# Low-part score products and prompt scores over all 128 rows of the TensorE array, in a two-layer hybrid attention step

## The chip, the cores and the metric

The kernel runs on one core of a Trainium2 chip. The metric is the device time of one execution in microseconds (us). TensorE (PE) multiplies matrices, VectorE (DVE), ScalarE (ACT) and GpSimd (POOL) work on elements, SyncE (SP) issues the DMAs. Every engine works through its own instructions in order and waits on semaphores of the others.

## The reference

One step of a two-layer network over 1024 sample tokens and 128 prompt tokens, 1024 wide. The part that matters here is the differential attention of four heads, each with two maps of 64 dims:

```
def _diff_attention(q, k, v, lam, subln_w, lam_init):
    s = jnp.einsum('bhqmd,bhkmd->bhmqk', q, k,
                   preferred_element_type=jnp.float32) * (HEAD_DIM ** -0.5)
    p = jax.nn.softmax(s, axis=-1)
    a = p[:, :, 0] - lam * p[:, :, 1]
    o = jnp.einsum('bhqk,bhke->bhqe', a, v.astype(jnp.float32))
    o = (o * lax.rsqrt(jnp.mean(jnp.square(o), axis=-1, keepdims=True) + RMS_EPS)
         * subln_w.astype(jnp.float32) * (1.0 - lam_init))
    return o.astype(v.dtype)
```

The samples' 1024 queries attend to 1152 keys (1024 of their own and 128 cached ones). The prompt's 128 tokens attend to themselves alone. Around it stand one input projection for all branches, a Fourier branch, a gated spatial branch, an output projection and a layer norm.

## The kernel before

Each layer has four stages: the start (normalization and first projections), the attention, the rest of the local branches, and the output projection. To keep the accuracy of 32-bit numbers at the faster rate of the rounded type, an operand is split into a rounded high part and a low part (the difference), and a product is made of three: high by high, high by low, low by high.

For the scores the two maps of 64 dims are laid out so that 128 rows hold two of these at once. K holds, for map 1, the high part in rows 0 to 63 and the low part in rows 64 to 127, and the other way round for map 2. `pack` prepares the queries of two tiles (256 queries) in a tile Q: ScalarE copies the high part of map m into both halves of Q[:, m] (L597 to L600), so that one product over 128 rows (L610) gives high by high and high by low. POOL then subtracts to get the low parts of both maps into one slice, Q[0:64, 2] and Q[64:128, 2] (L601, L602). The product low by high (L613) runs over the 64 rows of K that hold the high part.

`score` does this for one tile of 128 queries and one map: three products of 384 keys over 128 rows, then three over 64 rows, into the same PSUM tile S. VectorE takes the maximum (nm, L616) and ScalarE the exponentials (P, L618). With both maps there, `softmax_diff` joins them (POOL L562, DVE L563), `transpose` turns the result on PE (T, L628) and copies it (a, L631 and L632), and `values` multiplies by V (pv, L638). There are 2 layers x 4 heads x 8 tiles x 2 maps = 128 scores and 32 packs.

`prompt` runs once for each head. It has one product over 64 rows for each map (sp, L655), from qp and kp, which hold both maps one above the other.

PE's order is the order in which the code is written: `attention` is a generator, and between its steps `fill` and the streams put products of the input projection (z, L366), so that PE works while other engines finish. The other engines' orders are made by a scheduler with priorities. Rotation of a projected chunk of q or k uses tiles zz and sh (POOL L409, L410), K's low part is made by POOL (L419), weights' low parts by POOL (L347), the end of a head's rows in `finish_o` by POOL (msq, gs, L579 to L581) and DVE (L582). The next layer's modulation is summed by DVE (macc, L185) meanwhile.

Short-lived tiles share buffers by tags: tag "z" has three buffers, tag "Q" two.

Of the kernel before, what the change touches and what calls it, by code (L numbers as in the profile page):

```python
# [16 lines left out]
D = 1024  # L17
# [13 lines left out]
# PE time of other work that goes with each step of the attention of a head  # L31
# [15 lines left out]
# units of 128 columns of the input projection  # L47
# [3 lines left out]
# tags and counts of the short-lived tiles, by name  # L51
X_TAGS = {"wr": ("wraw", "woraw", "wada", "tabr", "mr", "ba"), "z": ("zz", "sh", "gt", "vT", "gmt", "gmg", "fot", "vs", "bd", "pqp", "ws", "kc", "vc", "Pp", "modacc"), "Q": ("Q", "bdr", "wsr", "h32"),
# [10 lines left out]
def backbone_step(ctx, tc, xs, xp, cT, w_ada, b_ada, w_in, w_out, ckT, cv, lamv, wf, wsT, bsT,  # L63
# [13 lines left out]
    # ---- tiles of the pools, by use  # L77
# [28 lines left out]
    # ---- constants  # L106
# [13 lines left out]
    cb = tX([128, 34], "cb")  # the conditionings; layer 0's biases of shift and scale; the subln weights  # L120
# [31 lines left out]
    # ---- adaLN modulation of one third (0 shift, 1 scale, 2 gate), for both conditionings  # L152
# [42 lines left out]
    # ---- layer norm over the free dimension of [128, D], in place  # L195
# [33 lines left out]
    def make_h(l, t, xn):  # L229
        """h^T of token tile t, split, from the normalized x [128 tokens, D]."""  # L230
# [20 lines left out]
    def make_h_pair(l, c, kp, xs3):  # L251
        """Two of the eight blocks of dims of h^T, for the three token tiles of a chunk."""
# [23 lines left out]
    def start(proj):  # L276
        """Layer 0's shift and scale by blocks of 256 dims; the first chunk of the input projection follows them."""
# [64 lines left out]
    # ---- weights  # L342
# [72 lines left out]
    def split_k(K, sl, src):  # L415
        # K[:, 0] = [hi of map 1; lo of map 1], K[:, 1] = [lo of map 2; hi of map 2]
# [82 lines left out]
    class Units:  # L499
        """A stream of dims-major units; the weights of the next ones are loaded ahead."""  # L500
# [9 lines left out]
        def gen(self, which, together=False, chunks=(0, 1, 2)):  # L510
            """The units one by one, or their chunks in turn."""
# [20 lines left out]
    class Stream:  # L532
        """Work to be interleaved with other work."""
# [14 lines left out]
        def until(self, *units):  # L548
            """Until these units are projected."""
# [8 lines left out]
    def softmax_diff(l, p1, p2, zz, name):  # L558
        """p1 <- p1 / z1 - lam * p2 / z2"""
# [10 lines left out]
    def finish_o(l, o, ms, sq, n, gs, sl):  # L570
        """gs[:, sl] <- RMS norm of o [128 dims, n tokens] * weight * gate"""
        pe.matmul(ms, lhsT=onesm, rhs=sq[:, :n], start=True, stop=True)
        dve.scalar_tensor_tensor(gs[:, sl], o, subs[:, l:l + 1], gs[:, sl], op0=ALU.mult, op1=ALU.mult)
        # r = (m + eps) ** -0.5 by logarithm, then a Newton step: r * (3 - (m + eps) * r * r) / 2
# [9 lines left out]
    # ---- attention: one pipeline over the heads and their tiles of 128 queries  # L584
    class Head:
# [7 lines left out]
        def pack(self, p):  # L593
            """Two tiles of queries: [hi; hi] of either map, and lo of both."""
            qr, qs = self.qr, slice(p * 256, p * 256 + 256)
            Q = self.Q = tX([128, 3, 256], "Q", F32R)
# [4 lines left out]
            pool.tensor_tensor(Q[0:64, 2], qr[0:64, qs], f(Q[0:64, 0]), op=ALU.subtract)  # L601
            pool.tensor_tensor(Q[64:128, 2], qr[64:128, qs], f(Q[64:128, 1]), op=ALU.subtract)  # L602
            return Q

        def score(self, Q, i, m, zz):
            S, K = psS(), self.K
            ql = slice((i % 2) * 128, (i % 2) * 128 + 128)
            r = slice(64 * m, 64 * m + 64)
            for n in range(3):
                pe.matmul(S[:, n, :CH], lhsT=Q[:, m, ql], rhs=K[:, m, n * CH:(n + 1) * CH],  # L610
                          start=True, stop=False)
            for n in range(3):
                pe.matmul(S[:, n, :CH], lhsT=Q[r, 2, ql], rhs=K[r, m, n * CH:(n + 1) * CH],  # L613
                          start=False, stop=True)
# [31 lines left out]
        def prompt(self):  # L646
            """The prompt attends to itself."""
# [3 lines left out]
            P = tX([128, 2, 128], "Pp")  # L651
            for m in range(2):
                S = psM((128, 128), "sp")
                r = slice(64 * m, 64 * m + 64)
                pe.matmul(S, lhsT=self.qp[r, :], rhs=self.kp[r, :], start=True, stop=True)  # L655
# [7 lines left out]
            aT = self.qp  # the queries are no longer needed  # L663
# [71 lines left out]
    # ---- the local branches  # L735
    def local_u(l):
# [6 lines left out]
        for ts in TG:  # L743
            z = yield from mm_tok(w, ts)
            t = tX([128, 2, 256], "gmt")[:, :len(ts)]
            g = tX([128, 2, 256], "gmg")[:, :len(ts)]
            silu_to(g, z, t)
            sl = ug[:, ts[0]:ts[-1] + 1]
            pool.tensor_tensor(sl, sl, g, op=ALU.mult)
# [22 lines left out]
    def local_f(l):  # L772
        ff = [tX((128, 4, 256), "ff") for _ in range(2)]
        fp = small([128, 1, 256], "fp", 1)
        res["f", l] = ff, fp
        w = load_w256(l, U_F)
        for ts in TG:
            z = yield from mm_tok(w, ts)
            t = ts[0] % 4
            act.activation(fp if ts[0] == 8 else ff[ts[0] // 4][:, t:t + 2], z, AF.Copy)  # L780
# [36 lines left out]
    def fourier_weights(l, j):  # L817
        """Block-diagonal channel DFTs times w_f, split: [hi, lo][cos, -sin]."""
# [25 lines left out]
    def fourier_prepare(l):  # L844
        """Sums and differences of the halves, tables and weights, all split."""
        ff, fp = res.pop(("f", l))
        # tables [hi, lo] of the odd and of the even frequencies
# [22 lines left out]
    def local_fourier(l):  # L870
# [4 lines left out]
        for j in range(2):  # L875
            cj = slice(j * 128, (j + 1) * 128)
            w, bd = fo[j], bdr[j]
            PQ = tW((128, 2, 2, 2, 256), "PQ")  # [hi, lo][cos, sin][even, odd]
            F = res["F", l, j] = tR(name="F")
            # the prompt  # L880
            sp_ = psS((128, 256), "dftp")
            pe.matmul(sp_, lhsT=fp[:, 0, cj], rhs=dftp, start=True, stop=True)
            pq = tX((128, 2, 256), "pqp", F32R)
            act.activation(pq[:, 0], sp_, AF.Copy)
            dve.tensor_tensor(pq[:, 1], sp_, f(pq[:, 0]), op=ALU.subtract)
# [13 lines left out]
            # the sine table's column of frequency 0 holds the cosines of frequency 512  # L899
# [5 lines left out]
            for q in range(2):  # L905
                for a, b in PASSES:
                    pe.matmul(uv[:, 2, 0:128], lhsT=bd[:, a, q], rhs=pq[:, b, q * 128:(q + 1) * 128],
# [9 lines left out]
            vs = tX((128, 2, 256), "vs")  # L917
            act.activation(vs, uv[:, 1].rearrange("p (e k) -> p e k", e=2), AF.Copy)
            act.activation(F[:, 512:513], uv[:, 2, 128:129], AF.Copy)
            act.activation(F[:, SEQ_S:], uv[:, 2, 0:128], AF.Copy)  # L920
            dve.tensor_tensor(F[:, 0:512].rearrange("p (k e) -> p e k", e=2), U, vs, op=ALU.add)
            dve.tensor_tensor(F[:, 1022:513:-2], U[:, 0, 1:], vs[:, 0, 1:], op=ALU.subtract)
            dve.tensor_tensor(F[:, 1023:512:-2], U[:, 1], vs[:, 1], op=ALU.subtract)
            dve.tensor_tensor(F, F, gsf[j], op=ALU.mult)

    def load_w_out(l):
        """The output projection's weights, split; in the order in which their places fall free."""
# [196 lines left out]
```

## Time and profile before

| | us |
|---|---|
| median of 3 runs | 1456.73 |
| lowest and highest | 1454.4 and 1459.6 |
| span of the profiled execution | 1457.9 |
| TensorE busy in it | 1386.1 |
| VectorE busy in it | 902.8 |
| GpSimd busy in it | 770.1 |
| ScalarE busy in it | 742.5 |

The profile gives the span of its one execution, from its first to its last instruction; the runs are timed apart from it. Busy times of the engines overlap, so they don't add up to the span. The mean granted clock of TensorE was 0.983 of full speed.

### The profile page before, as it was taken

What the parts mean: (1) busy time and instruction counts of PE and PEld (TensorE: products, weight loads), DVE (VectorE), ACT (ScalarE), POOL (GpSimd) and SP (SyncE); (2) the same over time, 40 slices, a digit from 0 to 9 for tenths busy, and PEclk for the clock granted to TensorE, in tenths of its full rate; (3) what the DMA queues carried; (4) which work ended last, traced back from release to release, by engine and by line L of the source; (5) the groups of instructions that cost most, each with busy time, mean ns of one, the idle gap of its engine ahead of it and who ended that gap; (6) DMA issues with size and microseconds to landing.
All of it is one profiled execution on the core that took longest, in us unless ns stands there. A gap on an engine that the chain in (4) does not pass through costs nothing.

```text
span 1457.9 us, 21131 instructions
## 1 busy us (share of the span) xinstructions
PE 1386.1 (95%) x8248; PEld 1220.4 (84%) x8248; DVE 902.8 (62%) x1351; ACT 742.5 (51%) x1370; POOL 770.1 (53%) x655
## 2 busy tenths in 40 slices
PE   7999999989899999999998999999899999999997
PEld 3688888888688899987888889888779999998787
DVE  5435566886867855345785555578765684434576
ACT  3466656556544345353556665665655544435321
POOL 2164665676563445236787675576574342533652
PEclk9999999999989999999999999999999999999999
DMA  9310011221221221354341100112100010126442
GB/s 340 136 34 31 19 33 46 65 74 32 81 70 32 88 62 50 107 187 149 123 157 46 50 21 29 48 33 89 62 33 7 25 46 30 35 84 211 151 130 91
DMA packets 56156, 114.42 MB, mean 78 GB/s; under 512 B 4972, under 2 KB 32492, under 8 KB 55928
## 3 DMA queue, kind: packets, MB, share of 16 engines
q1 hardware_dynamic: 56056, 113.07, 23.3%
q8 instruction: 65, 1.06, 0.3%
q14 instruction: 35, 0.29, 0.1%
HBM read 95.47 MB, written 17.58 MB: 78 GB/s over the span
## 4 chain that ended last, share of the span: by engine, by line
PE 69%; DVE 12%; ACT 6%; POOL 4%; issue 3%; DMA 2%; DVEq 0%; SPq 0%; POOLq 0%; ACTq 0%
PE z L366 21%; PE y L983 11%; PE zt L381 8%; PE pv L638 6%; PE S L613 5%; PE zt L386 4%; PE S L610 4%; PE T L628 3%; DVE macc L185 2%; PE dft L893 2%; DVE nm L616 1%; ACT P L618 1%; DMA wada<-in_w_ada_dram 1%; PE mres L191 1%; DVE rr L1000 1%
## 5 line engine op out<-in xcount | busy, mean ns | idle before, releaser
L366 PE MATMUL z<-H,w 128*128 128x384 f32 x2520 | 505.7, 348 | 15.7 <-DVE V L484 4.5
L366 PEld LDWEIGHTS z<-H,w 128*128 128x128 f32 x2520 | 437.4, 191 | 44.7 <-issue 26.5
L618 ACT ACTIVATE P<-S,nm 128x1152 f32<-128x1152 f32 x128 | 156.2, 1221 | 114.9 <-DVE nm L616 114.2
L616 DVE TENSOR_REDUCE nm<-S 128x1 f32<-128x1152 f32 x128 | 172.8, 1351 | 53.1 <-PE S L613 52.6
L381 PE MATMUL zt<-whi,H 128*128 128x256 f32 x1152 | 159.4, 286 | 2.3 <-ACT ug L741 2.1
L562 POOL TENSOR_SCALAR P<-P,rz,neglam 128x1152 f32<-128x1152 f32 x64 | 85.3, 1332 | 139.4 <-DVE rz L561 127.1
L381 PEld LDWEIGHTS zt<-whi,H 128*128 128x128 f32 x1152 | 145.6, 191 | 8.6 <-issue 5.2
L563 DVE SCALAR_TENSOR_TENSOR P<-P,rz 128x1152 f32<-128x1152 f32 x64 | 104.3, 1630 | 32.8 <-POOL P L562 32.6
L347 POOL TENSOR_TENSOR w<-wraw,w 128x1024 fp32r<-128x1024 f32 x36 | 91.5, 2541 | 59.0 <-ACT w L346 57.4
L638 PE MATMUL pv<-a,V 128*128 128x256 f32 x864 | 109.5, 284 | 5.1 <-ACT P L618 5.1
L638 PEld LDWEIGHTS pv<-a,V 128*128 128x128 f32 x864 | 106.9, 192 | 7.0 <-ACT P L618 7.0
L632 DVE TENSOR_TENSOR a<-T,a 128x1152 fp32r<-128x1152 f32 x64 | 86.6, 1353 | 36.4 <-ACT a L631 36.3
L613 PE MATMUL S<-K,Q 64*128 64x384 f32 x384 | 102.0, 372 | 0.0
L610 PE MATMUL S<-K,Q 128*128 128x384 f32 x384 | 91.1, 345 | 7.2 <-ACT P L618 3.4
L983 PE MATMUL y<-wob,mx 128*128 128x512 f32 (+1 forms) x342 | 87.0, 381 | 2.2 <-DVE rr L985 2.2
L613 PEld LDWEIGHTS S<-K,Q 64*128 64x128 f32 x384 | 60.8, 187 | 32.4 <-issue 29.4
L631 ACT ACTIVATE a<-T 128x1152 fp32r<-128x1152 f32 x64 | 72.3, 1130 | 28.3 <-PE T L628 27.4
L386 PE MATMUL zt<-wlo,H 128*128 128x256 f32 x576 | 83.3, 285 | 1.1 <-POOL wlo L347 1.1
L628 PE MATMUL T<-cs,P 128*128 128x128 f32 x576 | 74.8, 276 | 8.5 <-ACT P L618 8.5
L983 PE MATMUL y<-wo,mx 128*128 128x512 f32 (+1 forms) x342 | 80.5, 378 | 0.0
L628 PEld LDWEIGHTS T<-cs,P 128*128 128x128 f32 x576 | 67.6, 143 | 13.0 <-ACT P L618 9.2
L610 PEld LDWEIGHTS S<-K,Q 128*128 128x128 f32 x384 | 67.4, 191 | 12.9 <-ACT P L618 4.7
(215 smaller groups left out, 2374.9 us busy)
## 6 DMA issues: line engine op xcount, KB each, us to landing
wraw<-in_w_in_dram SPq DMA_DIRECT2D x52, 512.0 KB, 3.3
wada<-in_w_ada_dram SPq DMA_DIRECT2D x32, 512.0 KB, 3.7
wa<-in_w_ada_dram SPq DMA_DIRECT2D x8, 1024.0 KB, 12.4
woraw<-in_w_out_dram SPq DMA_DIRECT2D x16, 512.0 KB, 3.8
mr<-mix SPq DMA_DIRECT2D x18, 384.0 KB, 3.3
mix<-gs SPq DMA_DIRECT2D x8, 576.0 KB, 3.7
x<-rr SPq DMA_DIRECT2D x9, 512.0 KB, 3.2
xr<-x SPq DMA_DIRECT2D x9, 512.0 KB, 5.3
```

Source lines behind the costliest of these rows:

```text
L347: eng.tensor_tensor(lo, raw, f(hi), op=ALU.subtract)
L366: pe.matmul(z, lhsT=w[:, a, kt, :], rhs=Hc[c][:, b, kt, :], start=n == 0, stop=n == 23)
L381: pe.matmul(z[:, i, :], lhsT=Hc[c][:, a, kt, o:o + 128], rhs=w[0][:, kt, :], start=n == 0, stop=False)
L386: pe.matmul(z[:, i, :], lhsT=Hc[c][:, 0, kt, o:o + 128], rhs=w[1][:, kt, :], start=False, stop=kt == KT - 1)
L563: return dve.scalar_tensor_tensor(p1, p1, rz[:, 0:1], p2, op0=ALU.mult, op1=ALU.add)
L610: pe.matmul(S[:, n, :CH], lhsT=Q[:, m, ql], rhs=K[:, m, n * CH:(n + 1) * CH], start=True, stop=False)
L613: pe.matmul(S[:, n, :CH], lhsT=Q[r, 2, ql], rhs=K[r, m, n * CH:(n + 1) * CH], start=False, stop=True)
L616: dve.tensor_reduce(nm, S[:, :, :CH], axis=AX.XY, op=ALU.max, negate=True)
L618: act.activation(P.rearrange("p (c k) -> p c k", c=3), S[:, :, :CH], AF.Exp, bias=nm, accum_out=zz[:, m:m + 1])
L628: pe.transpose(T[:, kt // 3, kt % 3, :], a[:, kt * 128:(kt + 1) * 128], ident)
L638: pe.matmul(pv[:, 0, :], lhsT=self.V[:, a, kt, :], rhs=self.A[:, b, kt, :], start=kt == 0 and e == 0, stop=kt == 8 and e == 2)
L983: pe.matmul(z, lhsT=mx[:, a, k, :], rhs=wo[kt][b][:, ns], start=i == 0, stop=i == 23)
```

## The change

Q gets a fourth slice. The low part of each map is written into both halves of its own slice, by four POOL subtractions (L604) instead of two, and all six products of a score run over 128 rows (L613). The second three now also contain low by low, a term that was left out.

The prompt's queries get a tile qm of their own, in which each map's slice holds that map's 64 rows and zeros in the other 64: POOL clears it (L654) and copies the two halves (L657), and the products run over 128 rows of qm and kp (L660). qm takes a buffer of tag "z".

To make room, tiles of tag "z" shrink from 512 to 384 columns: gmt and gmg hold one token tile instead of two (nine groups of instructions instead of five), pqp and vs are split in two, fot moves to tag "Q", and the prompt's part of f goes into two small tiles.

```
         def pack(self, p):
...
-            Q = self.Q = tX([128, 3, 256], "Q", F32R)
+            Q = self.Q = tX([128, 4, 256], "Q", F32R)
...
-            pool.tensor_tensor(Q[0:64, 2], qr[0:64, qs], f(Q[0:64, 0]), op=ALU.subtract)
-            pool.tensor_tensor(Q[64:128, 2], qr[64:128, qs], f(Q[64:128, 1]), op=ALU.subtract)
+            for m in range(2):
+                r = slice(64 * m, 64 * m + 64)
+                for b in (0, 64):
+                    pool.tensor_tensor(Q[b:b + 64, 2 + m], qr[r, qs], f(Q[r, m]), op=ALU.subtract)
...
         def score(self, Q, i, m, zz):
...
-            r = slice(64 * m, 64 * m + 64)
-            for n in range(3):
-                pe.matmul(S[:, n, :CH], lhsT=Q[:, m, ql], rhs=K[:, m, n * CH:(n + 1) * CH],
-                          start=True, stop=False)
-            for n in range(3):
-                pe.matmul(S[:, n, :CH], lhsT=Q[r, 2, ql], rhs=K[r, m, n * CH:(n + 1) * CH],
-                          start=False, stop=True)
+
+            for e in (m, 2 + m):
+                for n in range(3):
+                    pe.matmul(S[:, n, :CH], lhsT=Q[:, e, ql], rhs=K[:, m, n * CH:(n + 1) * CH],
+                              start=e == m, stop=e != m)
...
         def prompt(self):
...
+            qm = tX([128, 2, 128], "qm")
+            pool.memset(qm, 0.0)
+            for m in range(2):
+                r = slice(64 * m, 64 * m + 64)
+                pool.tensor_copy(qm[r, m], self.qp[r])
             for m in range(2):
                 S = psM((128, 128), "sp")
-                r = slice(64 * m, 64 * m + 64)
-                pe.matmul(S, lhsT=self.qp[r, :], rhs=self.kp[r, :], start=True, stop=True)
+                pe.matmul(S, lhsT=qm[:, m], rhs=self.kp, start=True, stop=True)
...
     def local_u(l):
...
-            t = tX([128, 2, 256], "gmt")[:, :len(ts)]
-            g = tX([128, 2, 256], "gmg")[:, :len(ts)]
-            silu_to(g, z, t)
-            sl = ug[:, ts[0]:ts[-1] + 1]
-            pool.tensor_tensor(sl, sl, g, op=ALU.mult)
+            for i, t in enumerate(ts):
+                e, g = tX([128, 256], "gmt"), tX([128, 256], "gmg")
+                silu_to(g, z[:, i], e)
+                pool.tensor_tensor(ug[:, t], ug[:, t], g, op=ALU.mult)
```

The order of PE's instructions at the start of layer 0's attention, where z is the projection and S the score:

```order
 L366 MATMUL z<-H_113,w_592 128x384 x3
-L610 MATMUL S<-K,Q 128x384 x3
-L613 MATMUL S<-K,Q 128x384 x3
+L613 MATMUL S<-K,Q 128x384 x6
 L366 MATMUL z<-H_113,w_592 128x384 x6
-L610 MATMUL S<-K,Q 128x384 x3
-L613 MATMUL S<-K,Q 128x384 x3
+L613 MATMUL S<-K,Q 128x384 x6
```

The six products stay where the three and three stood.

POOL's order before the prompt of head 1 in layer 0, in the kernel before (Q from `pack`, sh and zz from the rotation, P from `softmax_diff`, K's low part, then `finish_o`):

```order
L601 TENSOR_TENSOR Q<-qr,Q 64x256
L602 TENSOR_TENSOR Q<-qr,Q 64x256
L409 TENSOR_TENSOR sh<-sh,rp 128x384
L410 TENSOR_TENSOR zz<-zz,rp 128x384
L562 TENSOR_SCALAR P<-P,rz,neglam 128x1152
L419 TENSOR_TENSOR K<-zz,K 64x384 x2
L409 TENSOR_TENSOR sh<-sh,rp 128x384
L410 TENSOR_TENSOR zz<-zz,rp 128x384
L579 TENSOR_TENSOR msq<-msq,sq 128x256
```

And the same place after the change:

```order
L604 TENSOR_TENSOR Q<-qr,Q 64x256 x4
L409 TENSOR_TENSOR sh<-sh,rp 128x384
L410 TENSOR_TENSOR zz<-zz,rp 128x384
L562 TENSOR_SCALAR P<-P,rz,neglam 128x1152
L419 TENSOR_TENSOR K<-zz,K 64x384 x2
L654 MEMSET qm 128x256
L409 TENSOR_TENSOR sh<-sh,rp 128x384
L410 TENSOR_TENSOR zz<-zz,rp 128x384
L657 COPY qm<-qp 64x128 x2
```

Two more subtractions stand ahead of everything, and the two copies of qm, for which the first sp on PE waits, stand behind the second rotation.

POOL's order at the start of layer 1's attention, in the kernel before (w is a weight unit's low part; K at the end is what the first score waits for):

```order
L601 TENSOR_TENSOR Q<-qr,Q 64x256
L409 TENSOR_TENSOR sh<-sh,rp 128x384
L410 TENSOR_TENSOR zz<-zz,rp 128x384
L602 TENSOR_TENSOR Q<-qr,Q 64x256
L347 TENSOR_TENSOR w_7327<-wraw,w_7327 128x1024
L601 TENSOR_TENSOR Q<-qr,Q 64x256
L409 TENSOR_TENSOR sh<-sh,rp 128x256
L410 TENSOR_TENSOR zz<-zz,rp 128x256
L602 TENSOR_TENSOR Q<-qr,Q 64x256
L347 TENSOR_TENSOR w_7688<-wraw,w_7688 128x1024
L419 TENSOR_TENSOR K<-zz,K 64x256 x2
```

And after the change:

```order
L604 TENSOR_TENSOR Q<-qr,Q 64x256 x2
L409 TENSOR_TENSOR sh<-sh,rp 128x384
L410 TENSOR_TENSOR zz<-zz,rp 128x384
L604 TENSOR_TENSOR Q<-qr,Q 64x256 x2
L347 TENSOR_TENSOR w_7413<-wraw,w_7413 128x1024
L604 TENSOR_TENSOR Q<-qr,Q 64x256 x2
L409 TENSOR_TENSOR sh<-sh,rp 128x256
L410 TENSOR_TENSOR zz<-zz,rp 128x256
L604 TENSOR_TENSOR Q<-qr,Q 64x256 x2
L347 TENSOR_TENSOR w_7778<-wraw,w_7778 128x1024
L419 TENSOR_TENSOR K<-zz,K 64x256 x2
```

Four more subtractions stand ahead of K; the rest has kept its order.

## Rows read from the trace of the kernel before

**Rows 1.** The page: span, busy time of each engine, chain by engine and line.
```profile
span 1457.9 us, 21131 instructions
...
PE 1386.1 (95%) x8248; PEld 1220.4 (84%) x8248; DVE 902.8 (62%) x1351; ACT 742.5 (51%) x1370; POOL 770.1 (53%) x655
...
PE 69%; DVE 12%; ACT 6%; POOL 4%; issue 3%; DMA 2%; DVEq 0%; SPq 0%; POOLq 0%; ACTq 0%
PE z L366 21%; PE y L983 11%; PE zt L381 8%; PE pv L638 6%; PE S L613 5%; PE zt L386 4%; PE S L610 4%; PE T L628 3%; DVE macc L185 2%; PE dft L893 2%; DVE nm L616 1%; ACT P L618 1%; DMA wada<-in_w_ada_dram 1%; PE mres L191 1%; DVE rr L1000 1%
```

**Rows 2.** Windows: length; PE, PEld, DVE, ACT, POOL busy; PE clock; DMA.
```profile
103.00:570.00 467.00, 447.96 (x2765) 399.12 (x2765) 322.60 (x452) 253.57 (x469) 252.51 (x216) 0.98 0.17 53
816.00:1262.00 446.00, 432.28 (x2727) 389.10 (x2726) 285.41 (x423) 245.50 (x459) 233.42 (x211) 1.00 0.12 37
317.20:320.60 3.40, 3.40 (x15) 3.40 (x13) 3.27 (x4) 3.34 (x7) 3.32 (x4) 0.50 0.00 0
846.60:850.00 3.40, 3.39 (x17) 2.90 (x18) 2.94 (x3) 1.75 (x5) 1.22 (x2) 1.00 0.00 0
```

**Rows 3.** Timeline of PE, layer 0: start, length, operation [wait before].
```profile
419.00 7.01 PE L366 MATMUL z<-H,w 128*128 128x384 f32 x39
425.85 0.68 PE L610 MATMUL S<-K,Q 128*128 128x384 f32 x3
427.19 2.35 PE L366 MATMUL z<-H,w 128*128 128x384 f32 x12
429.38 0.69 PE L610 MATMUL S<-K,Q 128*128 128x384 f32 x3
```

**Rows 4.** Timeline of PE at the prompt of head 1, layer 0.
```profile
248.52 1.15 PE L628 MATMUL T<-cs,P 128*128 128x128 f32 x9
249.60 0.48 PE L655 MATMUL sp<-kp,qp 64*128 64x128 f32 x2
250.01 1.83 PE L366 MATMUL z<-H,w 128*128 128x384 f32 x9
251.69 0.69 PE L610 MATMUL S<-K,Q 128*128 128x384 f32 x3
...
252.31 0.49 PE L655 MATMUL sp<-kp,qp 64*128 64x128 f32 x2
...
253.02 0.79 PE L366 MATMUL z<-H,w 128*128 128x384 f32 x3
```

**Rows 5.** Waits of PE, layer 0 and layer 1: us, times, longest.
```profile
PE T L628 <- ACT P L618: 4.2, 1, 4.2
...
PE pv L638 <- ACT P L618: 2.6, 3, 0.9
...
PE T L628 <- ACT P L618: 4.3, 1, 4.3
```

**Rows 6.** POOL's groups of instructions: count, busy us, mean ns, idle before.
```profile
L602 POOL TENSOR_TENSOR Q<-qr,Q 64x256 fp32r<-64x256 f32 x32 | 30.2, 945 | 6.8 <-ACT Q L599 3.8 <-ACT Q L600 1.7
L601 POOL TENSOR_TENSOR Q<-qr,Q 64x256 fp32r<-64x256 f32 x32 | 25.9, 811 | 77.3 <-ACT Q L597 77.3
L822 POOL MEMSET bd<- 128x256 f32 x4 | 1.2, 311 | 3.2 <-DVE gs L397 1.7 <-DVE fo L815 1.5
```

**Rows 7.** Timeline of POOL before that prompt.
```profile
245.33 1.30 POOL L562 TENSOR_SCALAR P<-P,rz,neglam 128x1152 f32<-128x1152 f32 x1 [0.82 <-DVE rz L561]
246.71 3.30 POOL L419 TENSOR_TENSOR K<-zz,K 64x384 fp32r<-64x384 f32 x2
...
251.06 1.02 POOL L410 TENSOR_TENSOR zz<-zz,rp 128x384 f32<-128x384 f32 x1
```

**Rows 8.** Timeline of POOL and of PE at the start of layer 1's attention.
```profile
814.71 2.40 POOL L347 TENSOR_TENSOR w<-wraw,w 128x1024 fp32r<-128x1024 f32 x1
817.19 1.53 POOL L419 TENSOR_TENSOR K<-zz,K 64x256 fp32r<-64x256 f32 x2
...
817.98 0.44 PE L610 MATMUL S<-K,Q 128*128 128x384 f32 x1 [0.57 <-POOL K L419]
```

**Rows 9.** Timeline of POOL, DVE and PE at a late T, layer 0.
```profile
302.42 1.61 POOL L602 TENSOR_TENSOR Q<-qr,Q 64x256 fp32r<-64x256 f32 x1
307.38 1.22 DVE L582 SCALAR_TENSOR_TENSOR gs<-msq,gs 128x256 f32<-128x256 f32 x1 [0.80 <-POOL msq L580]
308.52 5.36 DVE L185 SCALAR_TENSOR_TENSOR macc<-wada,csil,macc 128x1024 f32<-128x1024 f32 x2
316.55 1.62 PE L628 MATMUL T<-cs,P 128*128 128x128 f32 x9 [4.18 <-ACT P L618]
```

More of the change, by code (lines that the diff above doesn't have):

```diff
@@ L48 @@
 U_Q, U_K, U_V, U_G, U_F, U_GF, U_U, U_VM, U_GM = 0, 4, 8, 12, 16, 18, 20, 22, 24
-X_TAGS = {"wr": ("wraw", "woraw", "wada", "tabr", "mr", "ba"), "z": ("zz", "sh", "gt", "vT", "gmt", "gmg", "fot", "vs", "bd", "pqp", "ws", "kc", "vc", "Pp", "modacc"), "Q": ("Q", "bdr", "wsr", "h32"),
+X_TAGS = {"wr": ("wraw", "woraw", "wada", "tabr", "mr", "ba"), "z": ("zz", "sh", "gt", "vT", "gmt", "gmg", "vs", "bd", "pqp", "ws", "kc", "vc", "Pp", "qm", "modacc"), "Q": ("Q", "bdr", "wsr", "h32", "fot"),
           "sq": ("sq", "wft", "dftp", "msq", "bds", "cb")}
@@ L773, in local_f @@
         ff = [tX((128, 4, 256), "ff") for _ in range(2)]
-        fp = small([128, 1, 256], "fp", 1)
+        fp = [small([128, 128], n, 2) for n in ("qp", "kp")]
         res["f", l] = ff, fp
@@ L779, in local_f @@
             t = ts[0] % 4
-            act.activation(fp if ts[0] == 8 else ff[ts[0] // 4][:, t:t + 2], z, AF.Copy)
+            if ts[0] == 8:
+                for j in range(2):
+                    act.activation(fp[j], z[:, 0, j * 128:(j + 1) * 128], AF.Copy)
+            else:
+                act.activation(ff[ts[0] // 4][:, t:t + 2], z, AF.Copy)
     def local_gmlp(l):
@@ L881, in local_fourier @@
             sp_ = psS((128, 256), "dftp")
[L882 to L885, printed above, removed]
+            pe.matmul(sp_, lhsT=fp[j], rhs=dftp, start=True, stop=True)
+            pq = [tX((128, 256), "pqp", F32R) for _ in range(2)]
+            act.activation(pq[0], sp_, AF.Copy)
+            dve.tensor_tensor(pq[1], sp_, f(pq[0]), op=ALU.subtract)
             yield 500
@@ L906, in local_fourier @@
                 for a, b in PASSES:
-                    pe.matmul(uv[:, 2, 0:128], lhsT=bd[:, a, q], rhs=pq[:, b, q * 128:(q + 1) * 128],
+                    pe.matmul(uv[:, 2, 0:128], lhsT=bd[:, a, q], rhs=pq[b][:, q * 128:(q + 1) * 128],
                               start=n == 0, stop=n == 5)
@@ L916, in local_fourier @@
             U = uv[:, 0].rearrange("p (e k) -> p e k", e=2)
-            vs = tX((128, 2, 256), "vs")
-            act.activation(vs, uv[:, 1].rearrange("p (e k) -> p e k", e=2), AF.Copy)
+            vs = [tX((128, 256), "vs") for _ in range(2)]
+            for e in range(2):
+                act.activation(vs[e], uv[:, 1, e * 256:(e + 1) * 256], AF.Copy)
             act.activation(F[:, 512:513], uv[:, 2, 128:129], AF.Copy)
             act.activation(F[:, SEQ_S:], uv[:, 2, 0:128], AF.Copy)
-            dve.tensor_tensor(F[:, 0:512].rearrange("p (k e) -> p e k", e=2), U, vs, op=ALU.add)
-            dve.tensor_tensor(F[:, 1022:513:-2], U[:, 0, 1:], vs[:, 0, 1:], op=ALU.subtract)
-            dve.tensor_tensor(F[:, 1023:512:-2], U[:, 1], vs[:, 1], op=ALU.subtract)
+            for e in range(2):
+                dve.tensor_tensor(F[:, e:512:2], U[:, e], vs[e], op=ALU.add)
+            dve.tensor_tensor(F[:, 1022:513:-2], U[:, 0, 1:], vs[0][:, 1:], op=ALU.subtract)
+            dve.tensor_tensor(F[:, 1023:512:-2], U[:, 1], vs[1], op=ALU.subtract)
             dve.tensor_tensor(F, F, gsf[j], op=ALU.mult)
```

## Prediction

> **What bounds the kernel now.** I read the page's busy shares and its chain first. TensorE is busy for 95% of the span, the next engine for 62%, and 69% of the chain that ended last is TensorE's [rows 1]. The two score lines hold 9% of that chain (5 for L613, 4 for L610) and VectorE 12%. So in most places TensorE work taken away shortens the span, but at a wait for another engine it only lengthens the wait.
>
> Second come the windows of the two attentions, the only stages where the score runs. PE is busy 447.96 of 467 us in layer 0 and 432.28 of 446 us in layer 1, at a granted clock of 0.98 and 1.00 [rows 2]: 33 us of waiting in 913. POOL is at 54% and 52% there, with its order fixed, so any work ahead of an awaited operation counts in full.
>
> Third comes the score itself, in the timeline of PE [rows 3]. 39 products z of 384 columns take 425.85 − 419.00 = 6.85 us, or 0.1756 us each. The score right behind them has six products of the same 384 columns, three over 128 rows and three over 64, and takes 427.19 − 425.85 = 1.34 us, where six at the pace of z would take 1.05: 0.29 us too long. The twelve z behind it take 2.19 us where twelve at that pace take 2.11: another 0.08. So a score with its 64-row part costs about **0.37 us** more than six products of 128 rows, though no product has fewer columns. The time is lost at the two borders between 128-row and 64-row products, the second one partly charged to z. PE names no other engine here, and the clock is full.
>
> The Trainium skill, TensorEngine Tiling (Array Packing), "Key Properties", says that changing the tiling mode drains TensorE. The trace agrees: 0.37 us for two changes.
>
> **The change part by part.**
>
> *The score.* All six products become 128-row ones, in the same places of PE's order. Of 128 scores, 120 have nothing between their parts and save 0.37 us each: 44.4 us. The other 8 are those with the prompt's second product between the low parts [rows 4]: there it begins at 252.31, inside the score, and score and product together take 253.02 − 251.69 = 1.33 us, no more than a score alone. So today this 64-row product costs nothing. After the change the score takes 1.05 and the product its own time. The first product of the same prompt stands alone and takes 250.01 − 249.60 = 0.41 us, which is the upper bound; the lower is the 0.12 of a transposing product T of as many columns (nine from 248.52 to 249.60). So each of these 8 places gives between −0.13 and +0.16 us, and z behind it 0.08; the first products may save some 0.1 each by lost borders. I put +1 us for the whole prompt product. Gross: **45.4 us**.
>
> The Trainium skill, TensorE: Matmul & The Clock Gate, "Part 3: Packing small matmuls — row/col tiling", says that products in different row groups run side by side almost for free. The trace agrees for the prompt's second product, which speaks against that part of the change; for the low parts alone nothing runs beside them. By that page the prompt's edit would lose 8 products instead of gaining 1 us.
>
> *What the waits take back.* PE's waits in layer 0 are twelve rows with 20 waits, 19.1 us in sum, the largest a T for 4.2; in layer 1 eleven rows with 16 waits, 13.7 us [rows 5]. Where the wait is set by a chain through VectorE and ScalarE that starts at the end of an earlier score, the score between is hidden already: pv waits in this way for the exponentials of a first map while the second map's score lies between. Each of the 36 waits can swallow up to one score's 0.37: between 0 and 13.3 us. I take **−10**, near the upper end, since nearly all name ScalarE or VectorE.
>
> *POOL.* Q gets four subtractions for each pair of tiles instead of two: 64 more for 32 packs, at 0.81 or 0.95 us [rows 6], 56 us more on an engine with over 420 us free in the attentions. Mostly they lie in POOL's pauses. They cost time at three kinds of place.
>
> (a) *The prompt's mask.* The first sp no longer needs only qp: it waits for POOL's memset (the nearest row is another 128x256 memset, 0.31 us [rows 6]) and a copy of 64x128 elements (between that 0.31 and the 0.81 of a 64x256 subtraction; I take 0.5). In POOL's order (second piece above) they stand behind the rotation, and the copies last. Today at head 1 of layer 0 POOL is waiting for VectorE 0.82 us until 245.33, then runs without pause to the end of L410 at 251.06 + 1.02 = 252.08 [rows 7], and PE reaches sp at 249.60 [rows 4]. Two more subtractions push this by 1.6 less the pause of 0.82, so the mask would be ready at 252.1 + 0.8 + 0.3 + 0.5 = 253.7: up to 4.1 us late. Against this stands that the pair of K subtractions took 3.30 us here [rows 7] while smaller ones of 256 columns took 1.53 [rows 8]: stretched by other traffic, part of which moves away. I take 3.0 us, within 2.4 and 4.6. Heads 2 of layer 0 and 1 and 2 of layer 1 repeat this pattern; heads 0 and 3 have the copies early. Behind the waiting sp on PE stand z and the next score, so all engines wait: 4 × 3.0 = **−12** (−9.6 to −18.4).
>
> (b) *The first K.* In layer 1 the first score waits for POOL's K subtraction at 817.98 for 0.57 us, and POOL has come there through L347 without pause [rows 8]; four more subtractions (third piece above) with pauses of about 1 us taken off cost 2.2. Layer 0 has a looser start; between 0 and 2.2, I take 0.8. Together **−3** (−2 to −5).
>
> (c) *The two long waits for T.* POOL's Q (302.42, 1.61 us) precedes the msq for which VectorE waits until 307.38; behind that stand two additions of L185, 5.36 us, then the maximum on which T waits 4.18 us [rows 9]. Two more subtractions ahead push all of it by 1.5 us; layer 1 has the same with 4.3 [rows 5]. **−3** (0 to −4).
>
> *The clock.* After the wait for T the granted clock was 0.50 for 3.4 us, after the 1.54 us wait at 846.6 it stayed 1.00 [rows 2]. A stall of 3 us lies between the two. At half clock 3.4 us do the work of 1.7, so four such stalls cost between 0 and 6.8. **−4**.
>
> *The rest.* Smaller tiles for gmt and gmg, the moved fot, the halved pqp and vs: some 40 short instructions more on ScalarE, VectorE and POOL, beside TensorE's projections; more POOL time can also slow VectorE. **−2** (0 to −5). Eight new stalls give the other engines time to catch up, and the next of the old waits (33 / 36 = 0.9 us on average) shrinks by about 0.4: **+3**.
>
> Sum: 45.4 − 10 − 12 − 3 − 3 − 4 − 2 + 3 = 14.4 us. From the profiled 1457.9 us that is 1443.5; the median of the runs is 1.2 us lower, so **1442 us**.
>
> **The rivals.**
> 1. *POOL's work stays hidden*: the mask is ready in time because K's subtractions are not stretched, or the copies come early. Then (a) and most of the clock fall away: 1442 − 15 = 1427. For it: POOL's share of 54%. Against: the copies' place in the order.
> 2. *POOL eats the gain*: (a) at 4.6 each, the clock at 6.8, (b) at 5: 1442 + 6.4 + 2.8 + 2 = 1453; the lower end of "no change" begins at 1452.3.
> 3. *Slower: the lost 0.37 us is not the row change* but belongs to the second weight set or to accumulating into a written bank, and stays. Then nothing is gained and nothing taken back by the waits, and the costs of 22 us remain, less the 3: 1476. For it: no run shows a score of six full products. Against: sp, a 64-row product that accumulates into nothing, also takes 0.41 us where a T takes 0.12 [rows 4]. It decides from a remaining gap of 0.2 us in each score upward.
> 4. *Slower by VectorE and POOL getting in each other's way*: 56 us more POOL work makes the maximum and exponentials late at many tiles. It needs some 0.3 us for each of 64 tiles to reach 1461.
>
> **How the numbers follow.** Forecast (1434 to 1449): 0.46; rival 1 (1418 to 1434): 0.24; rival 2 (1449 to 1459): 0.18; rivals 3 and 4: 0.06 each. 0.3%, about what a measurement of this kernel tells from no change, is 4.4 us: faster means below 1452.3, slower above 1461.1. Faster: 0.46 + 0.24 + 0.04 of rival 2 = 0.74; same: 0.14 of rival 2 and 0.02 of rival 4 = 0.16; slower 0.10. The range leaves out rival 3, half of rival 4 and the tail of rival 1: 1422 to 1458.
>
> **What the profile of the changed kernel would show.** A score of six products at 1.05 us and z after it at its own pace confirm the gain. PE waits "<- POOL qm" of 2.4 to 4.6 us at four of the eight sp confirm (a), none at all rival 1. K's wait at layer 1's start should grow from 0.57 to about 2.8, the two waits for T by 1.5 each. PE's busy time should fall by about 45 us; if it falls by less than 20, rival 3 holds. The prediction is wrong if the copies on POOL land ahead of sp, or if the waits for VectorE swallow much more than 10.

## The result and the profile after

The change made the kernel slower: 1468.9 us against 1456.67, a ratio of 1.0078 (95% interval 1.0064 to 1.0093). I had forecast 1442, and the measured time lies outside the stated range of 1422 to 1458.

The page of the changed kernel: span, busy times, chain by engine, then by line.

```profile
span 1467.1 us, 21261 instructions
...
PE 1344.2 (92%) x8248; PEld 1241.2 (85%) x8248; DVE 908.1 (62%) x1363; ACT 747.3 (51%) x1400; POOL 832.6 (57%) x751
...
PE 57%; DVE 18%; POOL 8%; ACT 6%; DMA 4%; issue 3%; SPq 0%; DVEq 0%; POOLq 0%; ACTq 0%
```

TensorE does the same 8248 products in 41.9 us less than in [rows 1], and yet the span is 9.2 us longer. Its share of the chain fell from 69% to 57%, VectorE's rose from 12% to 18%, POOL's from 4% to 8%. The work got shorter, and the waits grew by 51 us (41.9 + 9.2).

The timeline of PE in the first scores of layer 0 (start, length, operation):

```profile
105.59 1.20 PE L613 MATMUL S<-K,Q 128*128 128x384 f32 x6
106.63 2.24 PE L366 MATMUL z<-H,w 128*128 128x384 f32 x12
108.71 1.20 PE L613 MATMUL S<-K,Q 128*128 128x384 f32 x6
```

A score takes 106.63 − 105.59 = 1.04 us and twelve z behind it 2.08; in [rows 3] it was 1.34 and 2.19. So each score gives 0.41 us: the gain that the prediction wrote down as 0.37 is there in full. That the time was lost at the borders, and not in the 64-row products themselves, stands in the kernel before, when narrow windows take the low products of the score of [rows 3] apart:

```profile
426.20 0.34 PE L610 MATMUL S<-K,Q 128*128 128x384 f32 x1
...
426.75 0.51 PE L613 MATMUL S<-K,Q 64*128 64x384 f32 x2
426.92 0.34 PE L613 MATMUL S<-K,Q 64*128 64x384 f32 x1
...
427.47 0.51 PE L366 MATMUL z<-H,w 128*128 128x384 f32 x2
```

The first low product starts at 426.47, the first z behind them at 427.19. From start to start, the last 128-row product takes 0.27 us and the first 64-row one 0.28; the second 64-row one takes 0.17, the pace of z; the last takes 0.27 and the first z 0.28.

Where it went stands in the list of PE's waits over the whole span (us, times, longest):

```profile
PE sp L660 <- POOL qm L657: 15.9, 4, 4.0
PE zt L381 <- DVE gmg L397: 12.1, 3, 6.2
PE T L628 <- ACT P L618: 7.3, 2, 3.8
...
PE z L366 <- DVE V L484: 6.7, 4, 3.6
...
PE z L366 <- DVE gs L397: 5.5, 2, 4.1
PE zt L381 <- ACT ug L746: 5.4, 3, 4.0
...
PE S L613 <- POOL K L419: 3.5, 1, 3.5
```

The first two rows are new. The mask of the prompt was expected; the gate gmg, one of the moves that only make room, was not. Laid side by side, PE instruction by PE instruction, the two traces show where. At 208 us of its own time the changed kernel is 10.7 us ahead: 0.5 of it from before the first score, 8.2 from the 20 scores up to there, and 3.2 from a stretch of half clock in the kernel before that has no counterpart (0.51 from 132.7 to 139.2 us), less some 1.2 taken back. Then it loses some 5.3 us at the sp of head 1 and as much at head 2; between 541 and 584 us of before, where the gates of local_u are projected, it falls from 5.0 ahead to 6.2 behind.

The timelines of POOL and PE at the prompt of head 1 in layer 0, the place of [rows 4, 7]:

```profile
234.82 1.31 POOL L562 TENSOR_SCALAR P<-P,rz,neglam 128x1152 f32<-128x1152 f32 x1 [0.77 <-DVE rz L561]
236.22 3.30 POOL L419 TENSOR_TENSOR K<-zz,K 64x384 fp32r<-64x384 f32 x2
239.57 0.31 POOL L654 MEMSET qm<- 128x256 f32 x1
239.96 1.00 POOL L409 TENSOR_TENSOR sh<-sh,rp 128x384 f32<-128x384 f32 x1
240.92 0.99 POOL L410 TENSOR_TENSOR zz<-zz,rp 128x384 f32<-128x384 f32 x1
241.86 0.86 POOL L657 COPY qm<-qp 64x128 f32<-64x128 f32 x2
...
237.05 1.15 PE L628 MATMUL T<-cs,P 128*128 128x128 f32 x9
242.20 0.49 PE L660 MATMUL sp<-kp,qm 128*128 128x128 f32 x2 [4.00 <-POOL qm L657]
```

This is the order forecast, with the copies last. K's pair still takes 3.30 us, so the relief that I had hoped for there did not come, and the wait is 4.0 us instead of 3.0. The two more subtractions did not push the mask here, though: POOL still waits 0.77 us for rz ahead of L562 (0.82 before), so they went into its pauses. Instead PE comes to sp sooner, 3.4 us behind the start of L562 (242.20 − 4.00 − 234.82) where it was 4.3 before (249.60 − 245.33). The clock behind these four stalls is in the windows (length; PE, PEld, DVE, ACT, POOL busy; PE clock; DMA):

```profile
103.00:570.00 467.00, 423.93 (x2747) 405.42 (x2747) 324.94 (x454) 253.38 (x477) 281.04 (x258) 0.97 0.17 53
816.00:1262.00 446.00, 414.87 (x2709) 402.42 (x2708) 285.81 (x426) 249.12 (x472) 266.91 (x260) 0.98 0.12 39
242.00:246.00 4.00, 3.80 (x14) 3.81 (x15) 1.27 (x3) 1.50 (x4) 3.79 (x6) 0.62 0.00 0
352.00:356.00 4.00, 3.58 (x13) 3.58 (x14) 0.51 (x2) 1.50 (x4) 3.71 (x6) 0.57 0.03 6
965.00:970.00 5.00, 4.61 (x18) 4.60 (x19) 1.32 (x3) 1.50 (x4) 4.71 (x8) 0.66 0.00 0
1075.00:1080.00 5.00, 4.30 (x16) 4.30 (x17) 1.22 (x3) 1.50 (x4) 4.56 (x8) 0.66 0.00 0
```

Each stall is followed by 1.5 to 1.7 us lost at the lower of the two levels: (1 − 0.62) × 4 = 1.5, (1 − 0.66) × 5 = 1.7. So one stall costs 4.0 us and up to 1.7 behind it, before anything is given back.

### The profile page after: what moved, and what is told of

It is laid out like the page before. It is cut to its first block, busy times and chain, and to the rows that moved or that the text cites. A ratio compares the mean times of both kernels' runs of the same rounds, so it can differ in the third digit from the quotient of the medians.

```text
span 1467.1 us, 21261 instructions
## 1 busy us (share of the span) xinstructions
PE 1344.2 (92%) x8248; PEld 1241.2 (85%) x8248; DVE 908.1 (62%) x1363; ACT 747.3 (51%) x1400; POOL 832.6 (57%) x751
## 4 chain that ended last, share of the span: by engine, by line
PE 57%; DVE 18%; POOL 8%; ACT 6%; DMA 4%; issue 3%; SPq 0%; DVEq 0%; POOLq 0%; ACTq 0%
PE z L366 18%; PE y L993 10%; PE S L613 7%; PE zt L381 6%; PE pv L638 4%; PE zt L386 3%; DVE nm L616 2%; DVE macc L185 2%; PE T L628 2%; POOL Q L604 2%; DVE P L563 2%; DMA wada<-in_w_ada_dram 2%; PE dft L901 2%; DVE vm L774 1%; DVE a L632 1%
## 5 line engine op out<-in xcount | busy, mean ns | idle before, releaser
L366 PE MATMUL z<-H,w 128*128 128x384 f32 x2520 | 499.8, 346 | 23.8 <-DVE V L484 6.7
L366 PEld LDWEIGHTS z<-H,w 128*128 128x128 f32 x2520 | 445.9, 193 | 30.2 <-DVE gs L397 6.2
L381 PE MATMUL zt<-whi,H 128*128 128x256 f32 x1152 | 161.9, 289 | 19.6 <-DVE gmg L397 12.1
L613 PE MATMUL S<-K,Q 128*128 128x384 f32 x768 | 161.8, 346 | 12.4 <-DVE a L632 4.6
L381 PEld LDWEIGHTS zt<-whi,H 128*128 128x128 f32 x1152 | 149.9, 196 | 22.0 <-DVE gmg L397 12.7
L613 PEld LDWEIGHTS S<-K,Q 128*128 128x128 f32 x768 | 137.7, 194 | 20.0 <-DVE a L632 6.7
L562 POOL TENSOR_SCALAR P<-P,rz,neglam 128x1152 f32<-128x1152 f32 x64 | 87.4, 1366 | 116.3 <-DVE rz L561 105.5
L604 POOL TENSOR_TENSOR Q<-qr,Q 64x256 fp32r<-64x256 f32 x128 | 107.4, 839 | 60.6 <-ACT Q L597 54.4
L563 DVE SCALAR_TENSOR_TENSOR P<-P,rz 128x1152 f32<-128x1152 f32 x64 | 110.5, 1726 | 32.4 <-POOL P L562 32.4
L386 PEld LDWEIGHTS zt<-wlo,H 128*128 128x128 f32 x576 | 75.0, 191 | 0.8 <-issue 0.8
```

The costliest lines, as they stand in the source:

```text
L381: pe.matmul(z[:, i, :], lhsT=Hc[c][:, a, kt, o:o + 128], rhs=w[0][:, kt, :], start=n == 0, stop=False)
L386: pe.matmul(z[:, i, :], lhsT=Hc[c][:, 0, kt, o:o + 128], rhs=w[1][:, kt, :], start=False, stop=kt == KT - 1)
L563: return dve.scalar_tensor_tensor(p1, p1, rz[:, 0:1], p2, op0=ALU.mult, op1=ALU.add)
L604: pool.tensor_tensor(Q[b:b + 64, 2 + m], qr[r, qs], f(Q[r, m]), op=ALU.subtract)
L613: pe.matmul(S[:, n, :CH], lhsT=Q[:, e, ql], rhs=K[:, m, n * CH:(n + 1) * CH], start=e == m, stop=e != m)
```

## The experiments

### One part of the change at a time

**a1** keeps queries, scores and prompt of before and makes only the room: the gates, as here, and the other moves of the change.

```
-            t = tX([128, 2, 256], "gmt")[:, :len(ts)]
-            g = tX([128, 2, 256], "gmg")[:, :len(ts)]
-            silu_to(g, z, t)
...
+            for i, t in enumerate(ts):
+                e, g = tX([128, 256], "gmt"), tX([128, 256], "gmg")
+                silu_to(g, z[:, i], e)
...
```

> The kernel before with only the moves that make room: gates and their temporaries by single token tiles, the split pqp and vs, fot in tag Q, f of the prompt in two small tiles. Queries, scores and prompt as before. Theory A (the small gate tiles cost time of their own, because each gate takes two of three buffers and TensorE waits for its multiplication on VectorE): 12 to 18 us slower than before, 1469 to 1475, with waits of PE zt for DVE gmg of 8 us or more. Theory B (those waits in the changed kernel only show that POOL and VectorE were late for other reasons): 1456 to 1460, and no such wait over 1 us.

1474.75 us, ratio 1.0110 (1.0088 to 1.0133): theory A. The list of PE's waits has at its top:

```profile
PE zt L381 <- DVE gmg L397: 11.9, 3, 6.0
```

How the longest comes about stands in ScalarE's timeline:

```profile
546.29 0.38 ACT L394 ACTIVATE gmt<-zt 128x256 f32<-128x256 f32 x1
549.03 1.06 ACT L346 ACTIVATE whi<-wraw 128x1024 fp32r<-128x1024 f32 x1 [2.35 <-DMA wraw<-in_w_in_dram]
549.99 0.40 ACT L395 ACTIVATE gmt<-gmt 128x256 f32<-128x256 f32 x1
550.30 1.11 ACT L631 ACTIVATE a<-T 128x1152 fp32r<-128x1152 f32 x1
551.31 0.40 ACT L396 ACTIVATE gmt<-gmt 128x256 f32<-128x256 f32 x1
```

This is the gate of a pair's second token tile. Its first exponential (L394) runs at 546.29, its logarithm only at 549.99: in ScalarE's order a weight's copy stands between, and that waits 2.35 us for its DMA. Then the copy of a T comes between, and VectorE multiplies at 554.0. All that time the pair's PSUM tile is held, and PE waits 6 us for it. Before, one gate served both token tiles, and at this pair its multiplication ended at 546.3.

**a2** is the change with the prompt of before, without qm.

```
...
-                pe.matmul(S, lhsT=qm[:, m], rhs=self.kp, start=True, stop=True)
+                r = slice(64 * m, 64 * m + 64)
+                pe.matmul(S, lhsT=self.qp[r, :], rhs=self.kp[r, :], start=True, stop=True)
```

> The changed kernel with the prompt's products over 64 rows of qp again, no mask. Theory A (the four waits for the mask cost 16 us, and the low clock behind each 1.7 more; borders around the 16 prompt products come back, some 0.3 us each): 17 to 20 us faster than the changed kernel, 1449 to 1452. Theory B (VectorE and ScalarE behind would make TensorE wait soon after anyway, the stalls are mostly given back): 0 to 8 us faster, 1461 to 1469.

1453.72 us, ratio to before 0.9984 (0.9967 to 1.0001), 15 us below the changed kernel: nearer to theory A. The mask turned "no change" into slower.

**a3** is the reverse, the mask in the kernel before.

> The kernel before with the mask and the prompt's products over 128 rows, nothing else. Theory A: the copies stand at the same place of POOL's order but two subtractions fewer ahead, so sp waits about 3.3 us at four heads and the clock falls after each: 15 to 20 us slower than before, 1472 to 1477. Theory B (the stalls need the extra subtractions, or are given back): 1457 to 1463.

1471.41 us, ratio 1.0093 (1.0070 to 1.0116), just below what theory A expected. The waits of sp for qm are 11.4 us in four, 3.0 the longest. Behind three of them the granted clock was 0.50, for 6.8 us from 249.5, 3.4 from 362.1 and 3.4 from 1078.9, which loses 6.8; behind the one of 2.81 us that ends at 967.2 it stayed 1.00. Together that is 18.2, so some 4 of it are given back. Without the earlier subtractions and the faster score the stall is 2.8 us in the mean, with them 4.0.

**a4** loads POOL alone.

```
-            pool.tensor_tensor(Q[0:64, 2], qr[0:64, qs], f(Q[0:64, 0]), op=ALU.subtract)
+            pool.tensor_tensor(Q[0:64, 2], qr[0:64, qs], f(Q[0:64, 0]), op=ALU.subtract)
+            pool.tensor_tensor(Q[0:64, 2], qr[0:64, qs], f(Q[0:64, 0]), op=ALU.subtract)
```

(and the same for the other map)

> The kernel before in which each of the two subtractions of a pack is done twice into the same place: POOL's extra load without any other part of the change. Theory A (POOL's load costs time only ahead of the first K of a layer and the two late T): 4 to 8 us slower, 1461 to 1465. Theory B (POOL's load slows VectorE everywhere): over 12 us slower, above 1469. Theory C (hidden): within 2 us of before.

1471.54 us, ratio 1.0096 (1.0070 to 1.0122): theory B by its number, but not by its mechanism. VectorE's maxima and exponentials are not late everywhere. The loss sits in three stretches, by the two traces side by side (times of before): 5.5 us between 410 and 504, 7.2 between 798 and 852, 3.7 between 1028 and 1196; some 4 us are given back in between. The second one is the first K of layer 1, in PE's timeline:

```profile
822.82 0.44 PE L612 MATMUL S<-K,Q 128*128 128x384 f32 x1 [2.24 <-POOL K L419]
```

and behind it the clock, in the windows:

```profile
822.00:828.00 6.00, 5.18 (x17) 3.87 (x18) 3.83 (x3) 1.31 (x2) 5.18 (x5) 0.72 0.25 87
828.00:840.00 12.00, 12.00 (x59) 10.96 (x59) 6.02 (x7) 7.34 (x14) 4.04 (x5) 0.85 0.16 51
```

Before, this wait was 0.57 us [rows 8] and the clock stayed at 1.00. Now it is 2.24, and the next 18 us lose 0.28 × 6 + 0.15 × 12 = 3.5 us of full clock. The first stretch holds PE waits for ScalarE's ug (2.9 us instead of 0.69) and VectorE's gs (1.8 instead of 0.2); the third holds smaller ones, of S for ScalarE's msq (1.2) and for gs (0.8 instead of 0.4).

### The score alone, and the load beside it

**d1** runs the second three products over 128 rows without any copy: slice 2 holds the low parts of both maps, and K's other half holds the low part of the keys, so each score gains only a product of two low parts (of the other map's queries with the own map's keys), of the size of the one that before leaves out.

```
-                pe.matmul(S[:, n, :CH], lhsT=Q[r, 2, ql], rhs=K[r, m, n * CH:(n + 1) * CH],
+                pe.matmul(S[:, n, :CH], lhsT=Q[:, 2, ql], rhs=K[:, m, n * CH:(n + 1) * CH],
```

> The kernel before in which the second three products of a score run over all 128 rows of the one slice that holds the low parts of both maps, without a copy: each score then also holds the product of the other map's low part of the queries with the own map's low part of the keys. Nothing changes on POOL, in the buffers or in the prompt. Theory A (the gain of the score was sized rightly, 47 us on PE, and the waits take 10 of it; the prompt's second product loses its free place, 3 us): 32 to 40 us faster than before, 1418 to 1426. Theory B (the waits take most of the gain, POOL and small tiles cost little beside it): 1440 to 1452.

1426.73 us, ratio 0.9795 (0.9762 to 0.9828): theory A, a little short of it, and the fastest of all kernels here. Its page:

```profile
span 1421.8 us, 21133 instructions
...
PE 1333.7 (94%) x8248; PEld 1227.9 (86%) x8248; DVE 903.7 (64%) x1351; ACT 741.5 (52%) x1370; POOL 776.9 (55%) x655
```

PE is busy 52.4 us less than before, and the span of this execution is 36 us shorter, so the waits take 16. By the medians of the runs it is 30 us shorter, and 22 are taken back. The two long waits for T alone are 11.2 us (8.5 before), and pv's 6.4 (5.1).

**d3** adds a4's doubled subtractions to d1.

> d1 with each POOL subtraction of a pack done twice, as in a4. Theory A (POOL's load costs as much beside the faster score as alone): 12 to 17 us above d1. Theory B (it costs more, since TensorE is ahead of POOL): 18 us or more. Theory C (less): under 8 us.

1443.61 us, ratio to before 0.9912 (0.9890 to 0.9934), 16.9 us above d1: theory A at its upper end. Alone the same load cost 14.5. Part of it is d3's own: all four subtractions write the one shared slice, and two scores wait for the last of them, 2.8 us each.

```profile
PE S L614 <- POOL Q L604: 5.6, 2, 2.8
```

PE has no such wait in the changed kernel, in a2 or in d2.

### Mending the gates

**b2** multiplies the gate in place, so that it needs one buffer instead of two, in a2.

```
-                e, g = tX([128, 256], "gmt"), tX([128, 256], "gmg")
-                silu_to(g, z[:, i], e)
+                e = tX([128, 256], "gmt")
+                silu_to(e, z[:, i], e)
...
```

> The changed kernel with the prompt over 64 rows, as in a2, and the gate multiplied in place, so that a token tile's gate takes one buffer of tag z instead of two. Theory A (the waits of PE zt for DVE gmg come from the two of three buffers that each gate holds): they go, 10 to 14 us faster than a2, 1440 to 1444. Theory B (they come from ScalarE standing behind a weight's load and from twice as many short instructions): at most 4 us faster than a2, 1449 to 1454.

1453.45 us, ratio 0.9968 (0.9949 to 0.9986), the same as a2 within 0.3 us. PE still waits 12.0 us for the gate in three waits. Buffers were not the cause; theory A falls.

**d2** computes the two gates of a pair in step.

```
+            es = [tX([128, 256], "gmt") for _ in ts]
+            for e, i in zip(es, range(len(ts))):
+                act.activation(e, z[:, i], AF.Exp, scale=-1.0)
+            for e in es:
+                act.activation(e, e, AF.Ln, bias=1.0)
+            for e in es:
+                act.activation(e, e, AF.Exp, scale=-1.0)
...
-                silu_to(g, z[:, i], e)
...
+                dve.tensor_tensor(es[i], z[:, i], es[i], op=ALU.mult)
...
```

> a2 (the change without the mask) with the two gates of a token pair computed in step: both first exponentials, both logarithms, both second exponentials, then both multiplications in place. Theory A (the second gate is late because ScalarE's order puts a weight copy and the copies of T between the two gates, and holds the PSUM tile that long): PE's waits for DVE gmt fall from 12 to under 3 us and the time by 10 to 14 us from a2, 1440 to 1444. Theory B (it is the number of short instructions): within 4 us of a2.

1435.69 us, ratio 0.9852 (0.9834 to 0.9869), 18 us below a2 and more than theory A expected. No wait for the gate is left. Here is ScalarE at a pair:

```profile
538.04 1.12 ACT L631 ACTIVATE a<-T 128x1152 fp32r<-128x1152 f32 x1
539.06 0.65 ACT L747 ACTIVATE gmt<-zt 128x256 f32<-128x256 f32 x2
539.59 0.73 ACT L749 ACTIVATE gmt<-gmt 128x256 f32<-128x256 f32 x2
540.20 0.73 ACT L751 ACTIVATE gmt<-gmt 128x256 f32<-128x256 f32 x2
```

The six instructions are as many and of the same size as in a2, 2.1 us together, but nothing stands between the first gate's and the second's. That rules out theory B: the order cost the time, not the number. It also bounds the rest: d2 holds all of the change but the mask and the old order of the gates, and lies 9.0 us above d1.

### Mending the mask and POOL's load

**b3** makes the mask with VectorE and ScalarE, on top of the gate in place.

```
-            pool.memset(qm, 0.0)
+            dve.memset(qm, 0.0)
...
-                pool.tensor_copy(qm[r, m], self.qp[r])
+                act.activation(qm[r, m], self.qp[r], AF.Copy)
```

> The gate in place, and the mask cleared by VectorE and copied by ScalarE instead of POOL; scores and prompt as in the change. Theory A (the mask was late only because POOL's rotation stands ahead of it): sp waits under 1 us, the borders of the prompt's products are saved, some 3 us below b2. Theory B (ScalarE's or VectorE's order has other work ahead of it): sp waits 2 us or more at four heads, 8 us or more above b2.

1463.66 us, ratio 1.0046 (1.0023 to 1.0070), 10 us above b2: theory B. The waits of sp are 8.3 us in four, 2.2 the longest, now for ScalarE. Half the stall is gone and the cost with the clock is two thirds of POOL's.

**b4** lets ScalarE make the second copy of the low part.

```
-                for b in (0, 64):
-                    pool.tensor_tensor(Q[b:b + 64, 2 + m], qr[r, qs], f(Q[r, m]), op=ALU.subtract)
+                o = slice(64 - 64 * m, 128 - 64 * m)
+                pool.tensor_tensor(Q[r, 2 + m], qr[r, qs], f(Q[r, m]), op=ALU.subtract)
+                act.activation(Q[o, 2 + m], f(Q[r, 2 + m]), AF.Copy)
```

> As b3, and the second copy of each low part is made by ScalarE from the first one, so POOL has two subtractions for a pack as before the change. Theory A (POOL's load cost some 14 us in a4 and costs as much in the change): 8 to 14 us below b3. Theory B (a wait of ScalarE for POOL takes its place): within 4 us of b3.

1466.06 us, ratio 1.0067 (1.0045 to 1.0089), 2.4 above b3: theory B. Two waits of PE have grown, from 7.4 and 4.0 in b3:

```profile
PE T L629 <- ACT P L619: 15.7, 4, 5.6
PE S L614 <- DVE a L633: 13.6, 9, 2.3
```

ScalarE waits 7.1 us in five waits for POOL's subtraction, and its 64 more copies take 0.42 us each, some 27 us; the exponentials and the copies of T behind both are late. Which of the two costs more was not told apart.

### Another cure for the borders

**c1** scores both maps of a tile together and lets the low products take turns.

```
...
+            for n in range(3):
+                for m in range(2):
+                    r = slice(64 * m, 64 * m + 64)
+                    pe.matmul(Ss[m][:, n, :CH], lhsT=Q[r, 2, ql], rhs=K[r, m, n * CH:(n + 1) * CH],
+                              start=False, stop=True)
...
```

> The kernel before with another cure: the two maps of a tile are scored together, six 128-row products, then the six 64-row ones in turn, rows 0 to 63 for map 1 and rows 64 to 127 for map 2. Nothing changes on POOL, in buffers or in the prompt; a first map's score comes some 1 us later. Theory A (64-row products of different rows run side by side, as the prompt's second product does in a score): each tile saves 0.9 us on PE, 58 us in all, of which the waits take 15 to 25, 1414 to 1425. Theory B (they don't, one border pair less for each tile is all): 24 us on PE, 1440 to 1448. Theory C (S1 coming sooner after T makes PE wait for its buffer): above 1450.

1477.63 us, ratio 1.0147 (1.0123 to 1.0172): theory C by the time, and theory A in the products on PE. PE's timeline at its first pair:

```profile
104.71 1.20 PE L610 MATMUL S<-K,Q 128*128 128x384 f32 x6
105.85 0.79 PE L615 MATMUL S<-K,Q 64*128 64x384 f32 x6
106.57 3.91 PE L366 MATMUL z<-H,w 128*128 128x384 f32 x21
```

and its waits:

```profile
PE T L633 <- ACT P L622: 58.0, 24, 5.1
PE pv L643 <- ACT P L622: 16.0, 20, 2.3
```

Six 64-row products take 106.57 − 105.85 = 0.72 us where six 128-row ones take 1.04: those of different rows do run side by side. PE's busy time falls from 1386.1 to 1346.6, less than theory A's 58 us and more than theory B's 24. But T now waits 58 us; it is T, and not the score as theory C has it (4.9 us), that waits for a buffer.

**c2** puts the pair at the place of the first score.

> c1 with the pair of scores at the place of the first one instead of the second, so that T has one step's products more between the pair and itself. Theory A (in c1 T waits for the PSUM tile that the late first score holds until its exponentials are read): T's waits fall from 58 us to under 25, the time to 1440 to 1455. Theory B (T waits for the chain of the tile before): T's waits stay above 45 us and the time above 1465.

1499.2 us, ratio 1.0291 (1.0269 to 1.0313). T's waits do fall to 15.3 us, as theory A says, but the time rises, which neither theory expected:

```profile
PE S L610 <- DVE a L637: 34.8, 25, 3.7
PE T L633 <- ACT P L622: 15.3, 8, 3.9
PE atp L667 <- ACT V L464: 13.6, 3, 4.6
```

S and T share two PSUM tiles (tag S). By the releasers in the two lists, T waits with the pair late until a score is read, and with the pair early the score waits until T's copies are made. What made the transposition of the prompt (atp) wait 13.6 us was not looked into.

## Why the prediction was wrong, point by point

The bound and the border were right. A score of six 128-row products saves 0.41 us, the prediction had 0.37; in d1 PE's busy time falls by 52.4 us where the term was 45.4. The Trainium skill, TensorEngine Tiling (Array Packing), "Key Properties", says that a change of tiling mode drains TensorE. The trace agrees: the four slow starts at the two borders, 0.41 us together, are gone with them. Rival 3 is ruled out. What the waits take back, −10, measured 16 in d1's profiled execution and 22 by the medians.

**The mask (a)** and its place behind the rotation were right, with the four heads named. The size was low: 4.0 us for a stall instead of 3.0. That it came so near to the unrelieved 4.1 is in part luck: at head 1 the push of 0.8 us by the subtractions was not there, and PE came 0.9 sooner, which the sum did not have. The clock was put at −4 and took 1.5 to 1.7 us behind each stall, 6.6 in all. Together −16 was predicted; a2 gives 15 and a3 14.4. The stalls and the clock behind them are 22.5 us in the change, so some 7 are given back; what gives them back was not followed.

**The step that failed is "The rest", −2 us (0 to −5).** It took the small tiles as a number of short instructions "beside TensorE's projections", so that they would cost PE next to nothing. a1 measures 17.7 us for the moves alone, and d2 gets 18.0 back from a2 by the order of the gates. What was missed is that two gates share one PSUM tile that PE needs back. Split into two chains in ScalarE's queue, the second came late, and PE waited 12.1 us in three waits. b2 and d2 tell the causes apart: it is not the buffers, nor the number, but the order. The prediction went by the orders of POOL and PE, and not by ScalarE's around the gates.

**POOL's load, terms (b) and (c), −6 us, was too small, by how much stays open.** d2 lies 9.0 us above d1, with the copies of the low parts and all moves but the gates' old order in it; the stand-ins that do each subtraction twice give more, 14.5 alone (a4) and 16.9 beside the faster score (d3, with a wait of its own). (b) was right in its mechanism: the wait for K is 3.53 us in the change, 2.96 more than before, for 2.2 predicted; but the low clock behind such a wait (0.75 for the 6 us from 827, 1.5 us lost) was not counted there, only for the mask. (c) was wrong in direction: the two long waits for T are 3.57 and 3.75 us, shorter than before [rows 5, 9]. The rest of POOL's cost appears as waits for ScalarE and VectorE at ug and gs; how POOL makes those late was not followed link by link.

**"+3" for shorter old waits** has no support: pv's waits are 5.2 us after and 5.1 before.

Two readings are off without moving the sum. The row of sp holds two matmuls (x2), so 0.41 us against 0.12 for one T compares two with one; in the change the second sp of that prompt takes 246.83 − 246.69 = 0.14 us. And rival 3's "costs of 22 us" are 24 by the prediction's own terms.

One step at a time from before, the parts add up by construction: score −30.2 (d1); the copies of the low parts and the moves other than the gates +9.0 (d2 above d1); the gates' order +18.0 (a2 above d2); the mask +15.2 (the change above a2); in sum +12.0. Of the 26.6 us between the forecast gain of 14.4 and the loss of 12.2, 16 are thus the term "The rest". The costs of the parts alone, 14.5, 17.7 and 14.4, make 46.6 where together they cost 42.2 beside d1; whether they overlap or the stand-in for POOL's load is too dear was not told apart. By its number rival 3 (1476) came nearest, but its mechanism is ruled out; rival 2 put the whole loss on POOL and ended at 1453.

## What to carry to other kernels

When TensorE changes between products of 64 and of 128 rows, look for the time at the border in the rows behind it too; it can be got back with no copies where the other rows hold something that may be added, as in d1. Cost the edits that "only make room" like the change itself: for each one ask which tile PE waits to get back, and read the order of the engine that frees it. A stall of a few us on TensorE can cost more than itself: behind most of those of 2 to 4 us here the clock was low for some us.

## What the runs showed of the hardware

- The change from 128-row to 64-row products and back costs 0.41 us in this kernel, of which 0.11 is charged to the products behind it; the 64-row product between others of its kind keeps the pace of the 128-row ones (0.17 us for 384 columns).
- 64-row products of different halves side by side: six of 384 columns in 0.72 us.
- After a wait of 2.24 us of PE the granted clock was 0.72 for 6 us and 0.85 for 12 more (a4); after one of 4.0 us it was 0.62 for 4 (the change); after one of 2.81 us it stayed 1.00 (a3).
- POOL clears a 128x256 tile in 0.31 us and copies 64x128 elements in 0.29 at the median, 0.51 in the mean and 1.33 at most (the change).
